# The last down block of eight experts: from 12 steps over 96 rows in the third part to 11 steps of 128 rows

## The chip, the cores and the metric

The kernel runs on one core of one Trainium2 chip. A core has TensorE (PE; its weight loads are listed apart as PEld), VectorE (DVE), ScalarE (ACT), GpSimd (POOL) and SyncE (SP), which here issues the transfers from HBM; 16 DMA engines move them. The metric is the device time of one execution in microseconds (us); the median of some runs is given. Inputs, weights and results are float32.

## The reference

Two transformer-like blocks follow each other on 256 tokens of width 1024. The first ends in 32 experts, the second holds two layers; the second of these ends in 8 experts of inner width 1408, two for each token, and only these matter here:

```python
def _swiglu(h, wg, wu, wd):
    return (jax.nn.silu(h @ wg) * (h @ wu)) @ wd

def _moe(h, router, wg, wu, wd):
    ...
    top_p, top_i = lax.top_k(probs, TOP_K_2)
    ...
    for e in range(N_EXPERTS_2):
        out = out + gates[:, e:e + 1] * _swiglu(hf, wg[e], wu[e], wd[e])
```

The kernel computes each expert only for the tokens that chose it.

## The kernel before

The program is one sequence of stages; the last one, `block2_moe` (from about 2340 us on), runs the 8 experts, with `moe_experts` (L979 on) as its loop. An expert has 96 places for tokens, in three groups of 32. Groups 0 and 1 always run. Group 2 stands under a condition (`tc.If`, L1081 and L1147) and runs only where an expert has more than 64 tokens; a branch jumps over its code otherwise. For an expert with more than 96 tokens there is `moe_rest`, which has the same arithmetic in other shapes and isn't entered in the profiled execution.

The inner width of 1408 is cut into four quarters of 352. A group's 32 tokens stand four times in the 128 columns of TensorE's array, one 32-column strip for each quarter (`tile_position=(0, 32 * q)`), so four products of 32 columns run side by side. For expert e the loop does:

- `gate_up` (L1058 on): gate and up products for each quarter, into `gu` (the first 256 of a quarter, L1071 with 512 moving columns) and `gub` (the remaining 96, L1071 with 192). Then the activation (L2268 to L2271) gives `a`, 128 x 3 x 352: row 32q + t is token t in quarter q.
- `combine(e - 2)` (L1041 to L1051): puts finished rows back to their tokens.
- `down(e - 1)` (L1119 on): the down products, L1140. The inner width is the contraction: a step takes one piece of one quarter, from `aT` as stationary and a row block `w` of down weights as moving operand, and issues four products, one for each 256 output columns. There are 8 steps with 128 rows (pieces 0 and 1 of the four quarters) and 4 with 96 rows (piece 2), so 12 for each group. The first four steps run for all groups, then the other eight.
- `turn(e)` (L1110 to L1117): transposes `a`, piece by piece, into PSUM (L1116) and copies it on ScalarE to `aT` (L1117); `aT` lies in `hTk`.

So experts are numbered from 0 here, and the down products of expert e stand after the gate and up products of expert e + 1.

Weights come in tiles through a ring of eight slots of 2 MB (`wtile`, L293 to L305, which issues the transfer). The slots are taken in a fixed order, so a transfer is issued when the last product on the tile eight places ahead is done. An expert takes nine tiles: gate and up in `wgu2` (four of 2 MB) and `wgu2b` (two of 1.5 MB, 128 rows of 12 KB), down in `wdn2` (two of 2 MB) and `wdn2b` (one of 1.5 MB: piece 2 of the four quarters, 96 rows of 16 KB). All are issued on SyncE's queue, in the order in which they are used. `load_dn` (L2278) lists the twelve steps: tile, block in the tile, quarter, piece.

Instructions of each engine are ordered by a scheduler when the program is built; the sections below show the places that matter. A float32 product stands as two passes in the trace, each with its weight load.

Of the kernel before, what the change touches and what calls it, by code (L numbers as in the profile page):

```python
# [13 lines left out]
AF = mybir.ActivationFunctionType  # L14
# [16 lines left out]
def host_layout(inp):  # L31
    f = lambda n: np.asarray(inp[n])
    c = np.ascontiguousarray
    o = {}
# [7 lines left out]
    w = f("w_in")[0]  # L42
# [21 lines left out]
    E = 32  # L64
# [11 lines left out]
    E = 8  # L76
# [2 lines left out]
    o["wgu2b"] = c(gu[..., 256:].reshape(E, 2, 4, 128, 768).transpose(0, 1, 3, 2, 4))  # L79
    wd = f("moe_w_down_2")[0].reshape(E, 4, 352, 1024)  # L80
    o["wdn2"] = c(wd[:, :, :256].reshape(E, 2, 4, 128, 1024).transpose(0, 1, 3, 2, 4))
    o["wdn2b"] = c(wd[:, :, 256:].transpose(0, 2, 1, 3))
    o["pos"] = c(f("positions_2").reshape(2, 128).T)
    w = f("w_in_2")
    rw = 1808
# [134 lines left out]
def bc(ap, shape):  # L220
    return ap.to_broadcast(shape)
# [71 lines left out]
def wtile(K, src, w=None):  # L293

    if w is None:
        if K.pre:
            return K.pre.pop(0)
        w = wslot(K)
    n = 1
    for s in src.shape[1:]:  # L300
        n *= s
    v = w[0:src.shape[0], 0:n]
    if len(src.shape) == 3:
        v = v.rearrange("p (a b) -> p a b", a=src.shape[1])
    K.nc.sync.dma_start(out=v, in_=src)  # L305
    return v
# [672 lines left out]
def moe_experts(K, pool, ps, mc, hs, cols, route, nE, F, load_gu, load_dn, bias, act, Y, cond, init):  # L979
# [4 lines left out]
    nc, tc = K.nc, K.tc  # L984
    nA = 256
    nB = F - nA
    pcs = [(0, 128), (128, 128)] + ([(256, nB)] if nB else [])
# [7 lines left out]
    two = 1 not in cond  # L995
# [57 lines left out]
    def start(p_, q, m, e=None):  # L1053

        l, r = (zl, bc(zl[:, 0:1], [96, m])) if e is None else (bc(bias[1][:, e:e + 1], [96, 32]), bias[0][:, 512 * q:512 * q + 512])
        nc.tensor.matmul(p_[32 * q:32 * q + 32, :], lhsT=l, rhs=r, start=True, stop=True, tile_position=(0, 32 * q))
# [53 lines left out]
    def turn(e):  # L1110
        a = st.pop(("a", e))
        aT = st["aT", e] = hTf[:, 0:384 * len(pcs)].rearrange("p (a b c) -> p a b c", a=len(pcs), b=3)
        for i, (o_, w_) in enumerate(pcs):
            pt = ps("x", [128, 3, 128])
            for g in range(3):
                nc.tensor.transpose(pt[0:w_, g, :], a[:, g, o_:o_ + w_], K.ident)  # L1116
            nc.scalar.activation(aT[0:w_, i], pt[0:w_], AF.Copy, scale=0.5)  # L1117

    def down(e):  # L1119
        aT = st.pop(("aT", e))  # L1120
        n = st.pop(("n", e))
        dn = load_dn(e)
        pd = [ps("d", [128, 2, 256]), ps("d", [128, 1, 256])]
        if bias is None:
            for p_, m in list(zip(pd, (512, 256)))[two:]:
                for c in range(4):
                    start(p_.rearrange("p a b -> p (a b)"), c, m)
        pd = [pd[0][:, 0], pd[0][:, 1], pd[1][:, 0]]
        if bias is not None:
            for g in range(3):  # L1130
                for c in range(4):
                    nc.tensor.matmul(pd[g][32 * c:32 * c + 32, :], lhsT=bc(bias[1][:, e:e + 1], [96, 32]),
                                     rhs=bias[2][c // 2][:, 256 * (c % 2):256 * (c % 2) + 256], start=g != 1, stop=True,
                                     tile_position=(0, 32 * c), skip_group_check=True)

        def part(g, dn, first):
            for k, (w, i, q, pi) in enumerate(dn):
                kk = pcs[pi][1]
                for c in range(4):
                    nc.tensor.matmul(pd[g][32 * c:32 * c + 32, :], lhsT=aT[0:kk, pi, g, 32 * q:32 * q + 32],  # L1140
                                     rhs=w[0:kk, i, 256 * c:256 * c + 256], start=first and two and g == 0 and k == 0, stop=True,
                                     tile_position=(0, 32 * c), skip_group_check=True)

        for n_, ds in enumerate((dn[:4], dn[4:]) if two else (dn,)):
            for g in range(3):
                if g in cond:
                    with tc.If(n > 32 * g):  # L1147
                        part(g, ds, n_ == 0)
                else:
                    part(g, ds, n_ == 0)  # L1150
        o = st["o", e] = [pool.tile([96, 1024], F32R, name=f"o{i}") for i in range(2)]
        rc = st["rc", e]
        of = pool.tile([96, 1024], F32, name="of") if nB else hTf[0:96, 1024:2048]
        for c in range(4):
            for g in range(3):
                dst, src, w_ = of[32 * g:32 * g + 32, 256 * c:256 * c + 256], pd[g][32 * c:32 * c + 32, :], rc[32 * g:32 * g + 32, 1:2]
                if g < 2:
                    nc.scalar.activation(dst, src, AF.Copy, scale=w_)  # L1158
                else:
                    nc.vector.tensor_scalar(dst, src, w_, None, op0=OP.mult)  # L1160
            if c % 2:
                c_ = slice(256 * c - 256, 256 * c + 256)
                if st["row"] is not None:
                    nc.vector.tensor_tensor(of[:, c_], of[:, c_], st["row"][0:96, c_], op=OP.mult)
                nc.scalar.activation(o[0][:, c_], of[:, c_], AF.Copy)  # L1165
                nc.vector.tensor_tensor(o[1][:, c_], of[:, c_], o[0][:, c_], op=OP.subtract)
# [4 lines left out]
    first = prep(0, range(4) if f32r else (0,))  # L1171
# [21 lines left out]
def moe_rest(K, pool, ps, h, cols, mc, posm, tgw, cnt, nE, F, wga, wgb, wda, wdb, bias, act, Y, row=None, after=None):  # L1193

    nc, tc = K.nc, K.tc
    nB = F - 256
    pcs = [(0, 128), (128, 128)] + ([(256, nB)] if nB else [])
# [3 lines left out]
    with tc.If(n > 96):  # L1201
        with tc.For_i(0, 2, 1):
            nc.vector.tensor_scalar(posm, posm, -96.0, None, op0=OP.add)
            with tc.For_i(0, nE, 1) as e:
# [14 lines left out]
                for q in range(2):  # L1219
                    px = ps("x", [128, 4, 96])  # L1220
                    for j in range(4):
                        for tt in range(2):
                            nc.tensor.matmul(px[:, j, :], lhsT=h[:, tt, 128 * (4 * q + j):128 * (4 * q + j) + 128], rhs=S[:, tt, 0, :],
                                             start=tt == 0, stop=tt == 1)
# [3 lines left out]
                a = pool.tile([96, 4, F], F32, name="a")  # L1228
                wa = [wtile(K, dyn(wga, e, i)) for i in range(4)]
                wb = [wtile(K, dyn(wgb, e, i)) for i in range(2)] if nB else []  # L1230
                for q in range(4):
# [9 lines left out]
                    if nB:  # L1241
                        pB = ps("gub", [96, 2 * nB])
                        for kt in range(8):
                            nc.tensor.matmul(pB, lhsT=xg[:, kt, :], rhs=wb[kt // 4][:, kt % 4, 2 * nB * q:2 * nB * q + 2 * nB],
                                             start=kt == 0, stop=kt == 7)
                        act(a[:, q, 256:F], pB[:, 0:nB], pB[:, nB:2 * nB], nB, 96)
                aT = hTf[:, 0:384 * len(pcs)].rearrange("p (a b c) -> p a b c", a=len(pcs), b=4)
                for i, (o_, w_) in enumerate(pcs):
                    pt = ps("x", [128, 4, 96])
                    for q in range(4):  # L1250
                        nc.tensor.transpose(pt[0:w_, q, :], a[:, q, o_:o_ + w_], K.ident[0:96, 0:96])
                    nc.scalar.activation(aT[0:w_, i], pt[0:w_], AF.Copy, scale=0.5)
                wd = [wtile(K, dyn(wda, e, i)) for i in range(2)]
                dn = [(wd[k // 4], k % 4, k // 2, k % 2, 128) for k in range(8)]
                if nB:
                    wl = wtile(K, dyn(wdb, e, None))
                    dn += [(wl, q, q, 2, nB) for q in range(4)]
                o = pool.tile([96, 1024], F32, name="of") if nB else hTf[0:96, 1024:2048]
                for c in range(2):
                    po = ps("d", [96, 512])  # L1260
                    for j, (w, i, q, pi, kk) in enumerate(dn):
                        nc.tensor.matmul(po, lhsT=aT[0:kk, pi, q, :], rhs=w[0:kk, i, 512 * c:512 * c + 512], start=j == 0,
                                         stop=j == len(dn) - 1)
                    o_ = o[:, 512 * c:512 * c + 512]
                    if row is None:
                        nc.scalar.activation(o_, po, AF.Copy)
                    else:
                        br = a.rearrange("p a b -> p (a b)")[:, 0:512]
                        nc.sync.dma_start(out=br, in_=bc(bias[1][bass.ds(e, 1), 512 * c:512 * c + 512], [96, 512]))
                        nc.vector.tensor_tensor(o_, po, br, op=OP.add)  # L1270
                        nc.vector.tensor_tensor(o_, o_, row[0:96, 512 * c:512 * c + 512], op=OP.mult)
# [10 lines left out]
def dyn(a, e, i):  # L1282

    if i is None:
        return a[bass.ds(e, 1)].rearrange("o p a b -> (o p) a b")
    return a[bass.ds(e, 1), i:i + 1].rearrange("o u p a b -> (o u p) a b")


def block1_moe(K, A):
# [65 lines left out]
    posm, tgw, num = moe_experts(K, pool, ps, mc, [h], mcol, route, 32, 256, load_gu, load_dn, (K.b3, K.oneh, bd), act, K.xres, (1, 2), row)  # L1355
    squares()
    moe_rest(K, pool, ps, h, mcol, mc, posm, tgw, num, 32, 256, A["wgu"], None, A["wdn"], None, (A["bgu"], A["bdn"]), act, K.xres, g2[0], squares)
    K.pend = [A["fnw"]]
    nc.vector.tensor_tensor(ssq, sq4[:, :, 0], sq4[:, :, 1], op=OP.add)
# [871 lines left out]
def block2_moe(K, A, out):  # L2231
    nc, tc = K.nc, K.tc
# [44 lines left out]

    def load_dn(e):  # L2278
        ws = [wtile(K, A["wdn2"][e, n]) for n in range(2)] + [wtile(K, A["wdn2b"][e])]
        return [(ws[k // 4], k % 4, k // 2, k % 2) for k in range(8)] + [(ws[2], q, q, 2) for q in range(4)]  # L2280

    moe_experts(K, pool, ps, mc, hs, K.lnc, route, 8, 352, load_gu, load_dn, None, act, Y, (2,), residual)
    moe_rest(K, pool, ps, K.xres, K.lnc, mc, *res, 8, 352, A["wgu2"], A["wgu2b"], A["wdn2"], A["wdn2b"], None, act, Y)
# [57 lines left out]
```

## Time and profile before

| | |
|---|---|
| median of 3 runs | 2742.53 us (2739.48 to 2747.18) |
| the profiled execution | 2748.39 us |
| its span, first to last instruction | 2746.6 us |
| TensorE busy | 2456.1 us (89% of the span) |
| VectorE, ScalarE, GpSimd busy | 1436.6, 935.7, 229.0 us |
| moved by DMA | 717.15 MB, 261 GB/s in the mean |
| TensorE's granted clock, mean | 0.953 of full speed |

The span is what the trace covers; 1.8 us of the profiled execution lie around it. An engine is busy while one of its instructions runs; matmuls are pipelined, so a busy TensorE needn't be at its peak. A pause is told with what ended it: another engine's instruction, a transfer (DMA), an engine's sequencer (PEq) or "issue", when nothing that the profile shows was waited for. DMA queue q1 carries the kernel's own transfers, q8 the packets of 16 KB with instructions.

### The profile page before, as it was taken

How to read it: one execution, taken by the hardware profiler on the slowest of the kernel's cores; microseconds unless marked ns; L12 is line 12 of the kernel's file. 1: busy time of each engine (PE TensorE's matmuls, PEld its weight loads, DVE VectorE, ACT ScalarE, POOL GpSimd, SP SyncE). 2: the span in 40 equal slices, each digit the busy share in tenths (PEclk: the TensorE clock that was granted, in tenths of full speed). 3: DMA queues.
4: the chain of work that ended last, by engine and by line, in shares of the span. 5: the costliest groups of instructions: out<-in, count | busy, mean ns of one | idle time of the engine just before them, and what ended most of it. 6: DMA issues, size and time to landing. Idle time of an engine off the chain costs nothing. (4 is left out here: it accounts for less than half of the span.)

```text
span 2746.6 us, 47587 instructions
## 1 busy us (share of the span) xinstructions
PE 2456.1 (89%) x20026; PEld 1610.0 (59%) x20026; DVE 1436.6 (52%) x2815; ACT 935.7 (34%) x1707; POOL 229.0 (8%) x222
## 2 busy tenths in 40 slices
PE   7999999988799989998997689879989987998895
PEld 4677668864344444443453278669987966554443
DVE  5888775554343454444343475775566577212223
ACT  4444344432132232222232362554444353021211
POOL 0422333110000000000000001110000030000000
PEclk9999999989999999999999799999999998999997
DMA  6333244759899999999999642345422225798994
GB/s 263 122 123 122 94 146 171 284 204 396 355 424 426 386 424 425 424 425 424 425 424 424 266 158 68 123 161 184 154 85 92 85 92 233 278 391 306 393 342 118
DMA packets 74282, 717.15 MB, mean 261 GB/s; under 512 B 9777, under 2 KB 25656, under 8 KB 29720
## 3 DMA queue, kind: packets, MB, share of 16 engines
q1 hardware_dynamic: 74008, 713.11, 66.1%
q8 instruction: 219, 3.59, 0.5%
q14 instruction: 55, 0.45, 0.0%
HBM read 712.03 MB, written 1.05 MB: 260 GB/s over the span
## 5 line engine op out<-in xcount | busy, mean ns | idle before, releaser
L1071 PE MATMUL gu<-w,xg 128*32 128x512 f32 x4400 | 539.7, 613 | 87.6 <-PEq L1081 48.0
L335 DVE TENSOR_TENSOR wlo<-w,whi 128x1024 fp32r<-128x1024 f32 (+1 forms) x250 | 309.1, 1238 | 206.5 <-ACT whi L334 205.4
L1071 PEld LDWEIGHTS gu<-w,xg 128*32 128x32 f32 x4400 | 157.2, 111 | 422.4 <-issue 369.8
L334 ACT ACTIVATE whi<-w 128x1024 fp32r<-128x1024 f32 (+1 forms) x250 | 260.7, 1045 | 380.9 <-PE pp L342 100.1
L1140 PE MATMUL d<-w,hTk 128*32 128x256 f32 (+1 forms) x5088 | 312.9, 392 | 30.7 <-issue 14.6
L1140 PEld LDWEIGHTS d<-w,hTk 128*32 128x32 f32 (+1 forms) x5088 | 178.8, 113 | 139.6 <-issue 53.8
L1330 DVE TENSOR_SCALAR a<-gu 128x256 f32<-128x256 f32 x96 | 39.5, 423 | 300.1 <-PE gu L1071 233.6
L1331 ACT ACTIVATE th<-a 128x256 f32<-128x256 f32 x96 | 36.6, 413 | 391.2 <-DVE a L1330 351.2
L1158 ACT ACTIVATE hTk<-d,rc 32x256 f32<-32x256 f32 x256 | 119.7, 468 | 79.3 <-PE d L1140 48.8
L1025 PE MATMUL x<-S,h 128*128 128x192 f32 (+2 forms) x608 | 110.7, 336 | 11.9 <-PEq L1147 4.9
L1049 PE MATMUL x<-o,R 96*128 96x512 f32 x320 | 95.5, 441 | 26.6 <-ACT o L1165 14.8
L1025 PEld LDWEIGHTS x<-S,h 128*128 128x128 f32 x608 | 99.0, 197 | 28.3 <-issue 18.2
L341 PE MATMUL pp<-big,whi 128*128 128x512 f32 (+2 forms) x296 | 110.0, 371 | 2.2 <-ACT big L473 2.2
L1117 ACT ACTIVATE hTk<-x 128x384 f32<-128x384 f32 (+1 forms) x88 | 41.0, 488 | 204.9 <-PE d L1140 138.6
L342 PE MATMUL pp<-big,whi 128*128 128x512 f32 (+2 forms) x296 | 109.4, 370 | 0.7 <-DVE big L474 0.5
L343 PE MATMUL pp<-big,wlo 128*128 128x512 f32 (+2 forms) x296 | 108.4, 367 | 0.0
L1049 PEld LDWEIGHTS x<-o,R 96*128 96x128 f32 x320 | 60.6, 203 | 73.7 <-issue 36.9
L341 PE MATMUL gu<-hT,whi 128*128 128x256 f32 x352 | 100.6, 286 | 1.9 <-ACT hT L2195 1.9
L343 PE MATMUL gu<-hT,wlo 128*128 128x256 f32 x352 | 100.5, 286 | 0.0
L342 PE MATMUL gu<-hT,whi 128*128 128x256 f32 x352 | 100.5, 286 | 0.0
L551 DVE SCALAR_TENSOR_TENSOR cacc<-pad,big,cacc 128x512 f32<-128x512 f32 (+1 forms) x128 | 98.0, 766 | 3.9 <-ACT cacc L548 1.2
L341 PE MATMUL pp<-whi,w 128*128 128x512 f32 (+1 forms) x192 | 81.3, 425 | 10.3 <-ACT w L2156 6.3
(734 smaller groups left out, 4701.6 us busy)
## 6 DMA issues: line engine op xcount, KB each, us to landing
w<-in_wgu_dram SPq DMA_DIRECT2D x155, 2048.0 KB, 22.7
w<-in_wdn_dram SPq DMA_DIRECT2D x80, 2048.0 KB, 25.9
w<-in_win_dram SPq DMA_DIRECT2D x18, 2048.0 KB, 7.9
w<-in_w2in_dram SPq DMA_DIRECT2D x30, 1024.0 KB, 5.2
w<-in_wgu2b_dram SPq DMA_DIRECT2D x16, 1536.0 KB, 15.3
w<-in_ffgu_dram SPq DMA_DIRECT2D x11, 2048.0 KB, 8.2
w<-in_wmod_dram SPq DMA_DIRECT2D x10, 2048.0 KB, 8.3
w<-in_wdn2b_dram SPq DMA_DIRECT2D x8, 1536.0 KB, 19.3
```

Source lines behind the costliest of these rows:

```text
L334: K.nc.scalar.activation(hi, src, AF.Copy)
L335: (eng or K.nc.vector).tensor_tensor(lo, src, hi, op=OP.subtract)
L341: K.nc.tensor.matmul(ps, lhsT=l[0], rhs=r[0], start=start, stop=False)
L342: K.nc.tensor.matmul(ps, lhsT=l[0], rhs=r[1], start=False, stop=False)
L343: K.nc.tensor.matmul(ps, lhsT=l[1], rhs=r[0], start=False, stop=stop)
L551: nc.vector.scalar_tensor_tensor(acc, pad[:, :S, k:k + 256], cw[:, ci, k:k + 1], acc, op0=OP.mult, op1=OP.add)
L1025: nc.tensor.matmul(px[:, j, :], lhsT=t_[:, tt, 128 * (q + j):128 * (q + j) + 128], rhs=S[:, tt, i:i + n].rearrange("p a b -> p (a b)"), st ...
L1049: nc.tensor.matmul(py, lhsT=R[:, 128 * tt:128 * tt + 128], rhs=o[i][:, 512 * c:512 * c + 512], start=i == 0, stop=i == 1)
L1071: mm = nc.tensor.matmul(p_[32 * q:32 * q + 32, :], lhsT=l_[:, kt, :], rhs=w[:, i, m * q:m * q + m], start=first, stop=True, tile_position= ...
L1117: nc.scalar.activation(aT[0:w_, i], pt[0:w_], AF.Copy, scale=0.5)
L1140: nc.tensor.matmul(pd[g][32 * c:32 * c + 32, :], lhsT=aT[0:kk, pi, g, 32 * q:32 * q + 32], rhs=w[0:kk, i, 256 * c:256 * c + 256], start=fi ...
L1158: nc.scalar.activation(dst, src, AF.Copy, scale=w_)
```

## The change

- On the host, the weights of the third pieces are laid out anew. Three quarters keep their 96 rows; the 96 rows of the fourth are cut into three blocks of 32, and each is put under one of the others. `wdn2b` becomes 128 rows of 12 KB instead of 96 rows of 16 KB, with the same bytes.
- `down` has 11 steps for each group, all of 128 rows.
- `turn` has to build the matching `aT`. The transposes of piece 2 stay, and their columns 96 to 127 (the fourth quarter) are no longer copied. For each group, three small products with 32 columns of `a` as stationary operand and 32 columns of the identity as moving operand put the fourth quarter's pieces into partitions 96 to 127, under the three others (`tile_position=(0, 96)`). The copy takes 128 x 3 x 96.
- `moe_rest` gets the same (left out below).

```diff
     o["wdn2"] = c(wd[:, :, :256].reshape(E, 2, 4, 128, 1024).transpose(0, 1, 3, 2, 4))
-    o["wdn2b"] = c(wd[:, :, 256:].transpose(0, 2, 1, 3))
+
+    o["wdn2b"] = c(np.concatenate([wd[:, :3, 256:], wd[:, 3, 256:].reshape(E, 3, 32, 1024)], 2).transpose(0, 2, 1, 3))
...
             pt = ps("x", [128, 3, 128])
             for g in range(3):
                 nc.tensor.transpose(pt[0:w_, g, :], a[:, g, o_:o_ + w_], K.ident)
-            nc.scalar.activation(aT[0:w_, i], pt[0:w_], AF.Copy, scale=0.5)
+                if i == 2:
+                    for j in range(3):
+                        nc.tensor.matmul(pt[96:128, g, 32 * j:32 * j + 32], lhsT=a[:, g, 256 + 32 * j:288 + 32 * j], rhs=K.ident[:, 96:128],
+                                         start=True, stop=True, tile_position=(0, 96))
+            c_ = 96 if i == 2 else 128
+            nc.scalar.activation(aT[:, i, :, 0:c_], pt[:, :, 0:c_], AF.Copy, scale=0.5)
...
             for k, (w, i, q, pi) in enumerate(dn):
-                kk = pcs[pi][1]
                 for c in range(4):
-                    nc.tensor.matmul(pd[g][32 * c:32 * c + 32, :], lhsT=aT[0:kk, pi, g, 32 * q:32 * q + 32],
-                                     rhs=w[0:kk, i, 256 * c:256 * c + 256], start=first and two and g == 0 and k == 0, stop=True,
+                    nc.tensor.matmul(pd[g][32 * c:32 * c + 32, :], lhsT=aT[:, pi, g, 32 * q:32 * q + 32],
+                                     rhs=w[:, i, 256 * c:256 * c + 256], start=first and two and g == 0 and k == 0, stop=True,
                                      tile_position=(0, 32 * c), skip_group_check=True)
...
-        return [(ws[k // 4], k % 4, k // 2, k % 2) for k in range(8)] + [(ws[2], q, q, 2) for q in range(4)]
+        return [(ws[k // 4], k % 4, k // 2, k % 2) for k in range(8)] + [(ws[2], q, q, 2) for q in range(3)]
```

The order on TensorE, second half of the down products of one expert, the transposes of the next one (piece 1 and 2) and the start of the gate products after it. `d` is the down sum, `x` the transposed piece, `gu` the gate and up sum; a row counts products, not passes; the row behind COMPARE_AND_BRANCH is group 2, which may be jumped over. Before:

```order
L1147 COMPARE_AND_BRANCH
L1140 MATMUL d<-w,hTk 32x256 x32
L1147 UNCONDITIONAL_BRANCH x2
L1140 MATMUL d<-w,hTk 32x256 x48
L1116 MATMUL x<-ident,a 128x128 x3
L1116 MATMUL x<-ident,a 96x128 x3
L1071 MATMUL gu<-w,xg 32x512 x32
L1081 COMPARE_AND_BRANCH
```

The same place in the changed kernel, where lines 1116 and 1140 are 1117 and 1145, and the small products line 1120:

```order
L1152 COMPARE_AND_BRANCH
L1145 MATMUL d<-w,hTk 32x256 x28
L1152 UNCONDITIONAL_BRANCH x2
L1145 MATMUL d<-w,hTk 32x256 x40
L1117 MATMUL x<-ident,a 128x128 x3
L1117 MATMUL x<-ident,a 96x128
L1120 MATMUL x<-ident,a 32x32 x3
L1117 MATMUL x<-ident,a 96x128
L1120 MATMUL x<-ident,a 32x32 x3
L1117 MATMUL x<-ident,a 96x128
L1120 MATMUL x<-ident,a 32x32 x3
L1072 MATMUL gu<-w,xg 32x512 x32
```

Each group has four down products fewer here (28 for 32 in group 2; 40 for 48 in the tail of group 0 and group 1), and three small products stand behind each transpose of piece 2. 

SyncE's queue, the tiles of two experts in turn (down of one, gate and up of the next but one). Before:

```order
L305 DMA w<-in_wdn_dram 128x4096
L1147 UNCONDITIONAL_BRANCH
L305 DMA w<-in_wdn2b_dram 96x4096
L305 DMA w<-in_wgu_dram 128x4096
L1147 UNCONDITIONAL_BRANCH
L305 DMA w<-in_wgu_dram 128x4096
```

In the changed kernel:

```order
L306 DMA w<-in_wdn_dram 128x4096
L1152 UNCONDITIONAL_BRANCH
L306 DMA w<-in_wdn2b_dram 128x3072
L306 DMA w<-in_wgu_dram 128x4096
L1152 UNCONDITIONAL_BRANCH
L306 DMA w<-in_wgu_dram 128x4096
```

The queue's order is the same; the block has 128 rows of 3072 elements instead of 96 rows of 4096.

## Rows read from the trace of the kernel before

**Rows 1.** Windows of 20 us: PE, PEld, DVE, ACT, POOL busy; clock, DMA share, GB/s.

```profile
2620.00:2640.00 20.00, 16.09 (x175) 8.00 (x177) 7.42 (x19) 1.27 (x4) 0.00 (x0) 0.76 0.99 277
2680.00:2700.00 20.00, 15.29 (x169) 7.97 (x168) 1.93 (x4) 3.19 (x7) 0.00 (x0) 0.74 0.94 254
```

**Rows 2.** Waits, TensorE alone, 2340 to 2705: total us, times, longest us.

```profile
PE d L1140 <- issue: 10.4, 5, 3.2
PE x L1049 <- issue: 7.3, 1, 7.3
...
PE d L1140 <- DMA w<-in_wdn2b_dram: 0.3, 1, 0.3
```

**Rows 3.** Timeline, TensorE: start us, us, work, count; in brackets the pause before it.

```profile
2440.12 2.25 PE L1049 MATMUL x<-o,R 96*128 96x512 f32 x8
...
2448.40 10.54 PE L1140 MATMUL d<-w,hTk 128*32 128x256 f32 x192
...
2487.32 3.57 PE L1049 MATMUL x<-o,R 96*128 96x512 f32 x8 [7.31 <-issue]
...
2491.01 6.70 PE L1140 MATMUL d<-w,hTk 128*32 128x256 f32 x96
...
2582.45 2.35 PE L1140 MATMUL d<-w,hTk 128*32 128x256 f32 x35 [0.64 <-DVE Y L1051]
2586.71 1.92 PE L1140 MATMUL d<-w,hTk 128*32 128x256 f32 x29 [1.91 <-issue]
...
2593.45 5.39 PE L1140 MATMUL d<-w,hTk 96*32 96x256 f32 x96 [2.42 <-PEq L1147]
...
2623.93 5.08 PE L1140 MATMUL d<-w,hTk 128*32 128x256 f32 x64 [1.76 <-DVE th L2270]
...
2633.01 0.64 PE L1140 MATMUL d<-w,hTk 128*32 128x256 f32 x7 [1.82 <-issue]
2633.94 8.60 PE L1140 MATMUL d<-w,hTk 96*32 96x256 f32 x96 [0.30 <-DMA w<-in_wdn2b_dram]
...
2680.17 2.42 PE L1140 MATMUL d<-w,hTk 128*32 128x256 f32 x32 [3.21 <-issue]
...
2688.48 8.64 PE L1140 MATMUL d<-w,hTk 96*32 96x256 f32 x96 [2.46 <-PEq L1147]
```

**Rows 4.** DMA view, 2471.9 to 2484.7 (its list of queues has only q1).

```profile
DMA packets 200, 2.80 MB, mean 219 GB/s; under 512 B 29, under 2 KB 29, under 8 KB 29
```

**Rows 5.** DMA view, 2484.7 to 2487.3: packets, MB, share of 16 engines' time.

```profile
q8 instruction: 1, 0.02, 3.2%
```

**Rows 6.** DMA view, 2382 to 2697, the instruction queue.

```profile
q8 instruction: 37, 0.61, 0.8%
```

**Rows 7.** Timeline, SyncE's queue, the block over 96 partitions of expert 3.

```profile
2528.63 0.33 SPq L305 DMA_DIRECT2D w<-in_wdn2b_dram  x1
```

**Rows 8.** DMA view, 2529.5 to 2537.3, the stretch after that issue.

```profile
DMA packets 130, 1.88 MB, mean 242 GB/s; under 512 B 15, under 2 KB 15, under 8 KB 15
```

**Rows 9.** DMA view, 2359.2 to 2362.9, a gate-up remainder (128 partitions, 12 KB).

```profile
DMA packets 130, 1.61 MB, mean 436 GB/s; under 512 B 16, under 2 KB 16, under 8 KB 16
```

**Rows 10.** DMA view, 2590.6 to 2593.4, while TensorE pauses for 2.42 us.

```profile
DMA packets 87, 1.18 MB, mean 420 GB/s; under 512 B 9, under 2 KB 9, under 8 KB 9
```

**Rows 11.** Lines, shapes apart: count, busy us, mean ns, idle before.

```profile
L1140 PE MATMUL d<-w,hTk 96*32 96x256 f32 x608 | 41.1, 406 | 5.4 <-PEq L1147 5.1 <-DMA w<-in_wdn2b_dram 0.3
...
L927 PE MATMUL x<-wr,hTk 128*128 128x32 f32 x32 | 3.8, 268 | 0.0
```

**Rows 12.** Timeline, TensorE, gate-up products and transposes in turn.

```profile
2521.71 0.55 PE L1116 MATMUL x<-ident,a 128*128 128x128 f32 x3
2522.19 1.06 PE L1071 MATMUL gu<-w,xg 128*32 128x512 f32 x8
2523.18 0.87 PE L1116 MATMUL x<-ident,a 128*128 128x128 f32 x6
2523.99 0.62 PE L1071 MATMUL gu<-w,xg 128*32 128x512 f32 x2
```

More of the change, by code (lines that the diff above doesn't have):

```diff
@@ L1249, in moe_rest @@
                     pt = ps("x", [128, 4, 96])
-                    for q in range(4):
+                    n_ = 3 if i == 2 else 4
+                    for q in range(n_):
                         nc.tensor.transpose(pt[0:w_, q, :], a[:, q, o_:o_ + w_], K.ident[0:96, 0:96])
-                    nc.scalar.activation(aT[0:w_, i], pt[0:w_], AF.Copy, scale=0.5)
+                        if i == 2:
+                            nc.tensor.matmul(pt[96:128, q, :], lhsT=a[:, 3, 256 + 32 * q:288 + 32 * q], rhs=K.ident[0:96, 0:96],
+                                             start=True, stop=True, tile_position=(0, 96))
+                    nc.scalar.activation(aT[:, i, 0:n_], pt[:, 0:n_], AF.Copy, scale=0.5)
                 wd = [wtile(K, dyn(wda, e, i)) for i in range(2)]
-                dn = [(wd[k // 4], k % 4, k // 2, k % 2, 128) for k in range(8)]
+                dn = [(wd[k // 4], k % 4, k // 2, k % 2) for k in range(8)]
                 if nB:
                     wl = wtile(K, dyn(wdb, e, None))
-                    dn += [(wl, q, q, 2, nB) for q in range(4)]
+                    dn += [(wl, q, q, 2) for q in range(3)]
                 o = pool.tile([96, 1024], F32, name="of") if nB else hTf[0:96, 1024:2048]
@@ L1260, in moe_rest @@
                     po = ps("d", [96, 512])
-                    for j, (w, i, q, pi, kk) in enumerate(dn):
-                        nc.tensor.matmul(po, lhsT=aT[0:kk, pi, q, :], rhs=w[0:kk, i, 512 * c:512 * c + 512], start=j == 0,
+                    for j, (w, i, q, pi) in enumerate(dn):
+                        nc.tensor.matmul(po, lhsT=aT[:, pi, q, :], rhs=w[:, i, 512 * c:512 * c + 512], start=j == 0,
                                          stop=j == len(dn) - 1)
```

## The prediction

> **What bounds the kernel now.** I read the windows of the last stage first (the second experts, from about 2340 us on), then TensorE's waits, then its timeline, then the DMA view in short stretches. Only differences in this stage count, since nothing ahead of it is touched.
>
> The windows show a stage in which the DMA engines are nearly full (shares 0.99 and 0.94) and TensorE is not: 16.09 and 15.29 us busy out of 20, at a mean granted clock of 0.76 and 0.74 [rows 1]. That looks like waiting for weights. The waits say otherwise: in 365 us TensorE waited 0.3 us for a weight transfer, but 10.4 us (5 times) and 7.3 us (once) under "issue", where nothing that the profile shows was missing [rows 2]. So weights are there in time, and something else stops it.
>
> The timeline shows where [rows 3]: pauses of 7.31, 1.91, 1.82 and 3.21 us under "issue", two of 2.42 and 2.46 us behind the branch of L1147, and 1.76 us ahead of the down products of expert 5 (2623.93), where expert 4 loses 0.64 us at the same place (2582.45). The pause of 1.91 us lies inside a run of equal products, after 35 of 64, where no operand changes. What ends such a pause is seen in the DMA view. In the 12.8 us up to 2484.7 the weight queue alone moved packets, and no instruction packet came [rows 4]; in the next 2.6 us exactly one did, of 0.02 MB, 3.2% of 16 engines' time, that is 1.3 us [rows 5], and TensorE went on at 2487.32. Over the stage 37 such packets came in 315 us, one in 8.5 us [rows 6]. I read this as: TensorE runs out of instructions, because the packet that brings the next ones stands behind weight packets on its DMA engine.
>
> Why there? The 1.5 MB block over 96 partitions is issued at 2528.63 [rows 7], and in the following 7.8 us the packets move 242 GB/s in the mean [rows 8]. A block of the same bytes over 128 partitions, the gate-up remainder, passes in 3.7 us at 436 GB/s [rows 9]. So a packet of the 96-partition block holds its engine about 1.8 times as long for its bytes, and what stands behind it waits longer. Stretches of the slow kind carry the long pause (219 GB/s in rows 4).
>
> **The change, part by part.**
>
> *The transfer.* Eight blocks take the shape of rows 9: 6.5 us (1.57 MB at 242 GB/s) or more become 3.7. The transfers themselves are no term, as weights are not waited for; the instruction packets behind them are. Pauses near such blocks: 7.31 + 1.91 + (1.76 - 0.64) + 1.82 + 3.21 + 2.46 = 17.8 us [rows 3]. [...] Its price comes from equal work at either level [rows 3]: 3.57 against 2.25 for the eight combining products; 6.70 against 5.39 for 96 down products (the latter at 2593.45); 5.08 against 3.59 (two thirds of 5.39); 8.60 and 8.64 against 5.39; 2.42 against 1.80: together 11.2 us. Both sum to 29.0 us.
>
> Not all of it goes. The pause of 2.42 us [rows 3] came while the DMA moved 420 GB/s [rows 10], and of the 10.4 us under "issue" 3.5 us lie outside slow stretches (10.4 - 1.91 - 1.82 - 3.21). I leave one pause of 2.4 us in experts 5 and 6 each, 4.8 us; after the one at 2593.45 the products ran at 5.39, full speed, so no clock loss is left with it. Back come 29.0 - 4.8 = **24.2 us**; as bounds, a third (9.7, if most of the waiting belongs to full queues of any packets) and all of it with the other pauses too (29.0 + 3.5 + 2.4 = 34.9).
>
> [...]
>
> *The removed step.* 19 of 24 expert groups run (608 / 32), and each loses one of four 96-row steps: 152 of 608 passes [rows 11]. At 10.54 us for 192 passes (0.055 us each) [rows 3] this takes 8.3 us from TensorE, all in its own chain.
>
> *The small products.* Three for each group, in all three groups of eight experts: 72 products. A product in float32 stands as two passes in the trace, so 144 passes of 32 columns. No row shows them. Below: 0.055 us, the rate of the column-tiled down passes; above: 0.119 us (3.8 / 32), 32 moving columns too, but with 128 columns of weights [rows 11]. These load 32, which is nearer to the first: 0.07 us, 10.1 us in all (bounds 7.9 and 17.1). They also alternate with full-width transposes. Three transposes take 0.48 us from start to the next product, six 0.81, so three more cost 0.33 and a change of layout there and back 0.15 [rows 12]. Two more such pairs for each expert: 2.4 us. [...]
>
> *The copy* of the third piece is 288 elements wide, not 384, on ScalarE, which stands outside TensorE's chain here; I count nothing. Nor does it cost if it comes to the front: a shorter copy takes the place of a longer one. *Issue order*: the queue of transfers keeps its order, row by row; only the shape differs. No wait is added. The last layer's tail, from 2705 on, loses its part of the removed passes, which is counted above.
>
> *Sum.* 24.2 back, 8.3 back, 10.1 and 2.4 spent: **20.0 us less**. The profiled execution, 2748.39 us, would become 2728; it lies 5.9 us above the median of the runs shown, and against that median, 2742.5, the forecast is **2722.5 us**.
>
> **The rivals.**
>
> *All pauses go.* With shorter transfers the queue is no longer full all the time, and instruction packets pass at once. For it: only slow stretches carry the pause of 7.31. Against: the 2.42 at 420 GB/s. With 34.9 back and the lower price of the products: 34.9 + 8.3 - 7.9 - 2.4 = 32.9, so 2709.6 us.
>
> *The pauses stay.* They belong to jumps over code that is not run (five groups are skipped) and to full queues, not to the block's shape. For it: two stand behind the branch of L1147. Against: 1.91 inside a straight run. Between none and a third comes back: 9.7 + 8.3 - 12.5 = 5.5 less, or 4.2 more: 2737 to 2747, say 2742. [...]
>
> *Slower: the products are dear.* All three of a group go to the same 32 columns and follow each other. If each pass must wait until the one before has left the array, it costs its whole duration, 0.268 us in the row with 32 moving columns [rows 11]: 38.6 us and 2.4 against 24.2 and 8.3, 8.5 us slower, 2751. It decides from 0.21 us a pass on ((24.2 + 8.3 - 2.4) / 144). Against it: the same row's passes follow at 0.119.
>
> *The change does not do what it says*: the block over 128 partitions stays slow, for its source rows are joined from two places. Rows 9 show this very shape at full rate, so I give it little; 2747.
>
> **How the numbers follow.** Chances: forecast 0.50, all pauses go 0.22, pauses stay 0.20, products dear 0.06, no effect on the transfer 0.02. Low end: all pauses go, 2709, and a little for unseen ones, 2708. High end: a third comes back with products at 0.119: 9.7 + 8.3 - 17.1 - 2.4, 1.5 us more, 2744. Beyond it lie the dear products and the worst part of "pauses stay". About 0.3%, 8.2 us, is what a measurement of this kernel can tell from no change. Faster by more: 0.50 + 0.22 and 0.04 from the edge of "pauses stay" = 0.76; slower by more: 0.06 and 0.01 of the last case = 0.07; the rest 0.17.
>
> **What would show it.** Right: the eight blocks move at over 400 GB/s; no pause over 3 us under "issue"; 20-us windows of the last experts with a granted clock near 1; 456 passes of the third kind of step, not 608. Steps wrong: blocks at full rate but the same pauses (the queue, not the shape); pauses gone but products at over 0.1 us a pass. The prediction is wrong if weights become what TensorE waits for, or if new pauses stand at the jumps.

## The result and the profile after

| | before | after |
|---|---|---|
| median | 2741.06 us (4 runs, 2739.48 to 2747.18) | 2712.14 us (4 runs, 2708.36 to 2715.85) |
| ratio to before | 1 | 0.9889 (95%: 0.9875 to 0.9903) |
| profiled execution, its span | 2748.39, 2746.6 us | 2715.85, 2713.9 us |

The changed kernel is 28.9 us faster by the medians, where 20.0 were forecast. The measured time lies inside the range, between the forecast (2722.5) and the rival "all pauses go" (2709.6). Lines moved a little: the down products of L1140 are L1145 now, the gate and up products L1072, the combining products L1050, the branch L1152, the small products L1120.

The windows that answer to [rows 1] (columns as there):

```profile
2480.00:2500.00 20.00, 18.67 (x205) 10.68 (x204) 6.95 (x17) 2.87 (x7) 0.00 (x0) 0.83 0.89 369
...
2600.00:2620.00 20.00, 18.96 (x293) 11.48 (x284) 8.26 (x21) 2.40 (x7) 0.00 (x0) 1.00 1.00 423
2620.00:2640.00 20.00, 19.59 (x252) 11.75 (x250) 1.38 (x2) 5.68 (x12) 0.00 (x0) 1.00 1.01 426
```

At 2620 TensorE is busy for 19.59 us of 20 instead of 16.09, its clock is granted in full instead of 0.76, and the DMA moves 426 GB/s instead of 277, at the same share of busy time. So the engines were no less busy before; they moved less.

TensorE's waits of the changed kernel, 2340 to 2672, against [rows 2] (total us, times, longest us):

```profile
PE d L1145 <- DVE Y L1052: 2.7, 4, 0.7
PE x L1050 <- ACT of L1163: 2.5, 1, 2.5
PE gub L1072 <- issue: 2.4, 1, 2.4
PE d L1145 <- issue: 1.7, 3, 1.2
PE d L1145 <- PEq L1152: 1.5, 5, 0.7
```

The 10.4 us of down products under "issue" are 1.7, the 7.3 us ahead of the combining products are gone, and the largest pause of that kind is one of 2.4 us, at 2479.67, at about the place of the former 7.31. Weights are still not waited for. In the timeline the down products of expert 4 behind the branch, formerly 2.42 us late [rows 3], are 0.19 late:

```profile
2577.56 0.55 PE L1117 MATMUL x<-ident,a 128*128 128x128 f32 x3
2578.04 0.27 PE L1057 MATMUL gub<-zl 96*32 96x192 bf16 x4
2578.13 1.90 PE L1145 MATMUL d<-w,hTk 128*32 128x256 f32 x32
2580.22 4.58 PE L1145 MATMUL d<-w,hTk 128*32 128x256 f32 x80 [0.19 <-PEq L1152]
2584.74 0.66 PE L1117 MATMUL x<-ident,a 128*128 128x128 f32 x4
2585.32 0.38 PE L1120 MATMUL x<-ident,a 128*32 128x32 f32 x6
2585.63 0.31 PE L1117 MATMUL x<-ident,a 128*96 128x128 f32 x1
2585.87 0.38 PE L1120 MATMUL x<-ident,a 128*32 128x32 f32 x6
2586.18 0.32 PE L1117 MATMUL x<-ident,a 128*96 128x128 f32 x1
2586.42 0.28 PE L1120 MATMUL x<-ident,a 128*32 128x32 f32 x3
2586.51 0.63 PE L1072 MATMUL gu<-w,xg 128*32 128x512 f32 x3
```

Behind it stand the new products, six passes, a transpose's pass, six passes again: from the first transpose to the next gate product 1.77 us, where six transposes alone took 0.81 [rows 12]. In the lines of 2280 to 2714, shapes apart (count, busy us, mean ns, idle before):

```profile
L1145 PE MATMUL d<-w,hTk 128*32 128x256 f32 x1672 | 99.1, 389 | 5.9 <-DVE Y L1052 2.7 <-issue 1.7 <-PEq L1152 1.5
L1120 PE MATMUL x<-ident,a 128*32 128x32 f32 x144 | 9.0, 200 | 0.0
```

1672 down passes are left of 1824 (608 of the third kind [rows 11] and 1216 others), 152 fewer, as counted; 144 small passes came. The 200 ns are the duration of one pass, not its pace: six took 0.38 us in the timeline above.

The block's own way in is told by the page's list of DMA issues (KB each, median us from issue to landing), before and after. It halves, though a landing holds the time in the queue too:

```profile
w<-in_wdn2b_dram SPq DMA_DIRECT2D x8, 1536.0 KB, 19.3
```

```profile
w<-in_wdn2b_dram SPq DMA_DIRECT2D x8, 1536.0 KB, 9.1
```

**One sum for all runs.** The stretch from the first to the last down product of these experts is called the stage here. From each trace I take its length, the sum of TensorE's pauses over 0.6 us, the part of them that ends 1.2 to 2.0 us after an instruction packet had come in, and the time at the lower granted clock (0.50 of full speed, as from 2488 to 2492 in the windows of the kernel before). Each is one execution. The one of the changed kernel was the longest of its four, and that of the kernel before lay 7.3 us above its median, so differences under 4 us or so are not read.

| kernel | stage | pauses | after an instruction packet | lower clock |
|---|---|---|---|---|
| before | 328.4 | 32.3 | 26.5 | 37.5 |
| after | 296.2 | 11.0 | 5.6 | 13.7 |
| e1 before, block padded | 305.0 | 18.3 | 12.5 | 13.7 |
| e2 after, block in 96 + 32 rows | 317.7 | 24.7 | 8.1 | 27.3 |
| e3 before, 4 KB packets | 325.6 | 33.4 | 25.5 | 30.7 |
| e4 after, no small products | 286.8 | 14.1 | 8.2 | 6.8 |
| e5 after, small products last | 291.7 | 11.8 | 5.3 | 10.2 |
| e7 after, half columns | 348.3 | 48.5 | 45.8 | 44.4 |
| e8 after, block padded | 298.0 | 12.8 | 6.8 | 10.2 |
| e9 after, block cut by rows | 317.0 | 27.1 | 10.5 | 20.5 |
| e10 after, block cut by columns | 292.5 | 10.5 | 5.5 | 6.8 |
| e11 after, cut by rows, partly interleaved | 316.5 | 21.6 | 11.9 | 27.3 |

At the lower clock equal work takes longer by 2.25 to 3.57 or 5.39 to 8.60 [rows 3], so 0.37 of that time is lost. The small products of expert 0 run ahead of the stage (from 2361 us on), so it holds those of seven experts. The change then reads: pauses 32.3 - 11.0 = 21.3 less, clock 23.8 x 0.37 = 8.8 less, removed passes 152 x 5.39 / 96 = 8.5 less, small products 7 x (1.77 - 0.81) = 6.7 more: 31.9 us less, of 32.2 measured in the stage.

### The profile page after: what moved, and what is told of

Read it like the earlier page. It is cut to its first block, busy times and chain, and to the rows that moved or that the text cites. A ratio compares the mean times of both kernels' runs of the same rounds, so it can differ in the third digit from the quotient of the medians.

```text
span 2713.9 us, 47571 instructions
## 1 busy us (share of the span) xinstructions
PE 2444.3 (90%) x20018; PEld 1626.4 (60%) x20018; DVE 1436.9 (53%) x2815; ACT 935.2 (34%) x1707; POOL 229.3 (8%) x222
## 3 DMA queue, kind: packets, MB, share of 16 engines
q8 instruction: 218, 3.57, 0.5%
## 5 line engine op out<-in xcount | busy, mean ns | idle before, releaser
L1072 PE MATMUL gu<-w,xg 128*32 128x512 f32 x4400 | 539.0, 612 | 87.9 <-PEq L1082 46.9
L1072 PEld LDWEIGHTS gu<-w,xg 128*32 128x32 f32 x4400 | 168.8, 111 | 409.1 <-issue 365.2
L1145 PE MATMUL d<-w,hTk 128*32 128x256 f32 x4936 | 295.2, 385 | 17.1 <-issue 6.3
L1145 PEld LDWEIGHTS d<-w,hTk 128*32 128x32 f32 x4936 | 172.6, 111 | 114.8 <-issue 32.6
L1026 PEld LDWEIGHTS x<-S,h 128*128 128x128 f32 x608 | 99.1, 197 | 28.7 <-issue 18.7
L1050 PE MATMUL x<-o,R 96*128 96x512 f32 x320 | 96.5, 443 | 18.3 <-ACT o L1170 14.8
L1050 PEld LDWEIGHTS x<-o,R 96*128 96x128 f32 x320 | 60.7, 205 | 66.7 <-issue 30.4
```

What stands on the lines that cost most here:

```text
L1026: nc.tensor.matmul(px[:, j, :], lhsT=t_[:, tt, 128 * (q + j):128 * (q + j) + 128], rhs=S[:, tt, i:i + n].rearrange("p a b -> p (a b)"), st ...
L1050: nc.tensor.matmul(py, lhsT=R[:, 128 * tt:128 * tt + 128], rhs=o[i][:, 512 * c:512 * c + 512], start=i == 0, stop=i == 1)
L1072: mm = nc.tensor.matmul(p_[32 * q:32 * q + 32, :], lhsT=l_[:, kt, :], rhs=w[:, i, m * q:m * q + m], start=first, stop=True, tile_position= ...
L1145: nc.tensor.matmul(pd[g][32 * c:32 * c + 32, :], lhsT=aT[:, pi, g, 32 * q:32 * q + 32], rhs=w[:, i, 256 * c:256 * c + 256], start=first an ...
```

## The experiments

All ratios are to the kernel before, run on the same chip.

**e1, the old kernel with a full-width block.** Only the transfer's shape changes: the 96 rows get 32 rows of zeros, so that 128 rows of 16 KB are fetched, a third more bytes. The steps stay twelve.

```diff
-    o["wdn2b"] = c(wd[:, :, 256:].transpose(0, 2, 1, 3))
+    o["wdn2b"] = c(np.pad(wd[:, :, 256:].transpose(0, 2, 1, 3), ((0, 0), (0, 32), (0, 0), (0, 0))))
```

> The kernel before, with all 12 steps and no small products, but its last down block is padded with 32 rows of zeros to 128 rows of 16 KB (2 MB), so that it moves in the fast shape. Theory A (instruction packets wait behind the slow packets of the 96-partition block, and TensorE runs dry and falls to the lower clock): pauses over 1 us nearly all go, granted clock near 1 in the last experts, some 28 us less than before, 2708 to 2718. Rival B (the gain came from TensorE's own work, 11 steps for 12): no change, 2737 to 2745. Rival C (the length of the weight transfers themselves counts): 4.9 us for the block in place of some 7.3, against 3.7 in the changed kernel, so about two thirds of the gain, 2719 to 2725.

Measured: 2723.76 us (2719.14 to 2727.11), 0.9928 (0.991 to 0.9946); 19.8 us of the 28.9. That is above the 2708 to 2718 of theory A and inside the 2719 to 2725 of rival C, which goes by the block's bytes; e8 below tests that. The shape is not all of the gain. More bytes went in less time: 11.9 us from issue to landing in the median, where it was 19.3. In the stage pauses fall by 14.0, all of it among those after instruction packets (26.5 to 12.5), and the lower clock takes 23.8 us x 0.37 = 8.8 less: 22.8 of the 23.4 us by which the stage is shorter. The 7.31 us became this (timeline of the padded kernel):

```profile
2474.70 1.84 PE L1071 MATMUL gub<-w,xg 128*32 128x192 f32 x40
2479.48 3.41 PE L1049 MATMUL x<-o,R 96*128 96x512 f32 x8 [2.95 <-issue]
```

Its windows show TensorE at its full clock, the DMA at 421 GB/s:

```profile
2620.00:2640.00 20.00, 17.96 (x246) 8.34 (x241) 1.38 (x2) 6.24 (x13) 0.00 (x0) 1.00 1.00 421
```

So the shape alone, with no change in the computation, carries about two thirds of the gain. What is left can be seen: 12.5 us of pauses after instruction packets are left, the changed kernel has 5.6.

**e2, the changed kernel with the block cut into 96 and 32 rows.**

```diff
-        ws = [wtile(K, A["wdn2"][e, n]) for n in range(2)] + [wtile(K, A["wdn2b"][e])]
+        ws = [wtile(K, A["wdn2"][e, n]) for n in range(2)] + [wslot(K)[:, 0:3072].rearrange("p (a b) -> p a b", a=3)]
+        for p in (slice(0, 96), slice(96, 128)):
+            K.nc.sync.dma_start(out=ws[2][p], in_=A["wdn2b"][e][p])
```

> The changed kernel, with 11 steps and small products, but its last down block (128 rows of 12 KB) is fetched by two transfers, 96 rows and then 32 rows. Theory A: both reach only some of the partitions and move slowly again, pauses behind them return, 2728 to 2742 (a packet is 12 KB here, not 16, so somewhat less than all). Rival B (11 steps for 12): stays at the changed kernel's time, 2709 to 2716. Rival C: as A.

Measured: 2733.91 us (10 runs, 2726.37 to 2748.92), 0.997 (0.9952 to 0.9988): two thirds of the gain by the medians, nearly three quarters by the ratios, are lost by this alone. Most of the loss has another form than before (TensorE's waits, 2340 to 2692):

```profile
PE d L1145 <- DMA w<-in_wdn2b_dram: 7.6, 2, 4.8
PE d L1145 <- issue: 4.9, 4, 2.2
```

Now the weights themselves are late, twice; before it was 0.3 us [rows 2]. Of the 13.7 us by which the pauses in the stage grow over the changed kernel's, only 2.5 end after an instruction packet. So the pauses that theory A expected came back only in small part; 7.6 us of waiting for the block came in their place. I read it so: TensorE comes to the block earlier, and the block is as slow as before (247 GB/s in the DMA view of 2525 to 2532, against 242 in [rows 8]). The slow block cost in two ways: in the kernel before 26.5 us of pauses after instruction packets and 0.3 us of waiting for it, here 8.1 us (5.6 in the changed kernel) and 7.6 us. That TensorE's pace decides between them is not shown by itself.

**e3, the old kernel with packets of 4 KB in place of 16 KB.** The block keeps its 96 rows and its bytes; if a number of packets ahead in the queue made the instructions late, four times as many would change it.

```diff
-    o["wdn2b"] = c(wd[:, :, 256:].transpose(0, 2, 1, 3))
+    o["wdn2b"] = c(wd[:, :, 256:])
...
-        return a[bass.ds(e, 1)].rearrange("o p a b -> (o p) a b")
+        return a[bass.ds(e, 1)].rearrange("o q p b -> p (o q) b")
...
-        ws = [wtile(K, A["wdn2"][e, n]) for n in range(2)] + [wtile(K, A["wdn2b"][e])]
+        ws = [wtile(K, A["wdn2"][e, n]) for n in range(2)] + [wtile(K, A["wdn2b"][e].rearrange("q p b -> p q b"))]
```

> The kernel before, with 12 steps and the 96-partition block, whose rows are laid out in HBM by quarter, so that one transfer has four packets of 4 KB for each partition in place of one of 16 KB. Theory A, if an instruction packet waits for a number of packets ahead of it: the block stays slow (200 to 250 GB/s), but the wait behind it is a quarter as long, pauses go, 2710 to 2722. If it waits for the block's bytes whatever their packets: pauses stay, 2735 to 2745. Rival C (length of the transfer): 2735 to 2745 with the pauses of before. Rival B: 2737 to 2745.

Measured: 2743.96 us, 0.9999 (0.9985 to 1.0013), no change. The block passes at the old rate (DMA view, 2470 to 2480; 219 GB/s in [rows 4]), and the long pauses stand where they stood, 6.4 us the longest:

```profile
DMA packets 416, 2.19 MB, mean 219 GB/s; under 512 B 25, under 2 KB 25, under 8 KB 368
```

The pauses sum up to 33.4 us, against 32.3 before. So here it didn't matter into how many packets the block's bytes were cut; they moved at the same rate, and the pauses stayed.

**e4 and e5, the small products.** e4 leaves them out, and with them the last 96 channels of the fourth quarter from the sums. e5 issues all nine behind the three transposes instead of three behind each. Their edits:

```diff
-                if i == 2:
-                    for j in range(3):
-                        nc.tensor.matmul(pt[96:128, g, 32 * j:32 * j + 32], lhsT=a[:, g, 256 + 32 * j:288 + 32 * j], rhs=K.ident[:, 96:128],
-                                         start=True, stop=True, tile_position=(0, 96))
...
-            nc.scalar.activation(aT[:, i, :, 0:c_], pt[:, :, 0:c_], AF.Copy, scale=0.5)
+            nc.scalar.activation(aT[0:w_, i, :, 0:c_], pt[0:w_, :, 0:c_], AF.Copy, scale=0.5)
```

```diff
             for g in range(3):
                 nc.tensor.transpose(pt[0:w_, g, :], a[:, g, o_:o_ + w_], K.ident)
-                if i == 2:
+            if i == 2:
+                for g in range(3):
                     for j in range(3):
```

> The changed kernel without the 72 small products (it leaves out placing the fourth quarter's last 96 channels). The prediction's price for them, 10.1 + 2.4 us: 2700. By the changed kernel's trace (passes 0.03 us apart, but a change of layout of over 0.1 us at each side of a transpose) some 9 us: 2701 to 2705. If they are hidden beside other work: 2709 to 2714.

> The changed kernel with the nine small products of an expert behind its three transposes of the third piece, not three behind each: two changes of layout there and back less for each expert. The changed kernel's trace has some 0.13 us more at each change between them: 0.5 us an expert, 4 us in all, 2706 to 2710. The prediction's 0.15 us a pair: 2.4 us less, about 2710. If a change of layout costs nothing by itself: 2712.

Measured: e4 2707.5 us (2702.92 to 2709.36), 0.9861 (0.9845 to 0.9878); e5 2705.49 us (2703.5 to 2712.1), 0.9852 (0.9835 to 0.9868). e4 lies between its two cases (2701 to 2705, and 2709 to 2714 if the products were hidden), e5 just below its 2706 to 2710. Moving the products brings as much as leaving them out, within the intervals, and e5 is the fastest kernel of this study that computes all. Its timeline shows the same place as above:

```profile
2581.30 0.88 PE L1117 MATMUL x<-ident,a 128*128 128x128 f32 x6
2582.11 0.66 PE L1121 MATMUL x<-ident,a 128*32 128x32 f32 x15
2582.58 0.63 PE L1072 MATMUL gu<-w,xg 128*32 128x512 f32 x3
2582.60 0.26 PE L1121 MATMUL x<-ident,a 128*32 128x32 f32 x3
```

From the first transpose to the next gate product it is 1.28 us, not 1.77. The eighteen passes cost 1.28 - 0.81 = 0.47 us, 0.026 us each. They start 0.03 us apart (fifteen in 0.66 us, at 0.20 us for one), but the last three stand beside the first gate products. The two further pairs of layout changes in the changed kernel cost the other 0.49, 0.24 us a pair. Eight times over that is 3.8 us for the passes and 3.9 for the order.

**e7, twice as many instructions for the down products.** Each is cut into two of 128 columns. The weights, their transfers and the arithmetic stay, and each product still has its own weight load (3344 passes and 3344 loads in the lines). The sums lie 0.069 off (relative), for a reason that no run shows.

```diff
-                for c in range(4):
-                    nc.tensor.matmul(pd[g][32 * c:32 * c + 32, :], lhsT=aT[:, pi, g, 32 * q:32 * q + 32],
-                                     rhs=w[:, i, 256 * c:256 * c + 256], start=first and two and g == 0 and k == 0, stop=True,
+                m = 256 if bias is not None else 128
+                for o_, c in [(o_, c) for o_ in range(0, 256, m) for c in range(4)]:
+                    nc.tensor.matmul(pd[g][32 * c:32 * c + 32, o_:o_ + m], lhsT=aT[:, pi, g, 32 * q:32 * q + 32],
+                                     rhs=w[:, i, 256 * c + o_:256 * c + o_ + m], start=first and two and g == 0 and k == 0, stop=True,
```

> The changed kernel with each down product of the second experts cut into two of 128 columns: the same arithmetic and the same transfers, twice the instructions in the down steps. Theory A (TensorE runs out of instructions, whose packets wait in full queues): long pauses come back in every expert, ended by instruction packets, 2735 to 2780. If pauses come from weights or from branches, not from the supply of instructions: passes of 128 columns follow each other at no less than 0.03 us, so the work does not grow, 2705 to 2720.

Measured: 2765.73 us (2764.56 to 2769.82), 1.0079 (1.0062 to 1.0095), 53.6 us above the changed kernel. The products themselves take 115.7 us instead of 99.1, part of it at the lower clock; but in front of them stand 43.2 us of pauses under "issue" and the branch (lines, 2280 to 2763):

```profile
L1146 PE MATMUL d<-w,hTk 128*32 128x128 f32 x3344 | 115.7, 299 | 45.9 <-issue 27.9 <-PEq L1153 15.3 <-DVE Y L1052 2.5
```

In its timeline TensorE stops in the middle of equal products:

```profile
2396.28 5.08 PE L1146 MATMUL d<-w,hTk 128*32 128x128 f32 x128 [3.50 <-issue]
2403.32 3.78 PE L1146 MATMUL d<-w,hTk 128*32 128x128 f32 x127 [1.95 <-issue]
2409.36 2.35 PE L1146 MATMUL d<-w,hTk 128*32 128x128 f32 x38 [2.26 <-issue]
```

In the stage, pauses rise by 37.5 and the lower clock by 30.7 x 0.37 = 11.4 us, 48.9 of 52.1. Data, transfers and multiplications are the same, only the number of instructions changed, and 45.8 of the 48.5 us of pauses ended 1.2 to 2.0 us after an instruction packet: I read these pauses as a lack of instructions. 128 and 127 passes stand between the pauses above, each pause ended by one more packet; they took 5.08 and 3.78 us.

The records of the packets, each with its start, say how far apart they come. In e7 the packets that ended pauses over 1 us ahead of or inside runs of down products started 5.6 to 8.9 us after the one before (the first and the last of these pauses aside), while the DMA moved 381 to 438 GB/s. In the kernel before, those that ended the pauses of 7.31, 1.91, 1.82, 3.21 and 2.46 us came 13.9, 10.2, 9.5, 16.4 and 9.0 us after the one before, at 205 to 278 GB/s. 128 passes of 256 columns take 7.2 us (at 5.39 us for 96). So at the full rate a packet came about as often as 128 of these are done, and too seldom for passes of 128 columns (5.08 and 3.78 us for 128 and 127); at the slow rate of the kernel before it came too seldom for passes of 256 columns as well. That a packet stands behind weight packets on its engine is not shown, as the traces don't name the engine of a packet; that the packets came further apart where the queue moved slower is.

Pauses of this kind came even with next to no weights to move. Towards the end of e7's stage, with the DMA at a share of 0.02, a packet came 3.0 us after the one before and still ended a pause (window and timeline):

```profile
2704.00:2710.00 6.00, 4.95 (x143) 4.08 (x138) 2.43 (x6) 0.06 (x1) 0.00 (x0) 1.00 0.02 5
```

```profile
2710.73 3.48 PE L1146 MATMUL d<-w,hTk 128*32 128x128 f32 x118 [1.60 <-issue]
```

**e8, the changed kernel with the block padded to 2 MB.** e1 fetches a third more bytes than the changed kernel and keeps more pauses. Are the bytes the reason?

```diff
+    o["wdn2b"] = c(np.pad(o["wdn2b"], ((0, 0), (0, 0), (0, 1), (0, 0))))
```

> The changed kernel, its block padded with a fourth, unused column block to 128 rows of 16 KB (2 MB): the transfer of the padded kernel with 11 steps. If the transfer's bytes made the padded kernel's remaining pauses (rival C in its weaker form: fuller queues): pauses over 0.6 us as there (18.3 us), 2717 to 2723. If they come from the longer code of 12 steps: as the changed kernel, 2709 to 2715.

Measured: 2716.13 us (2711.67 to 2720.56), 0.9893 (0.9875 to 0.9912), as the changed kernel and a little above the 2709 to 2715 expected for that. Not the bytes, then, and rival C falls. What e1 alone has among the kernels whose block moves at full rate is the twelfth step: it keeps 12.5 us of pauses after instruction packets, the five with eleven steps (after, e4, e5, e8, e10) 5.3 to 8.2, with the small products or without.

**e9, e10, e11: what makes the block slow.** e9 cuts the changed kernel's block by rows in another way for each expert (64 + 64, 96 + 32, 112 + 16, four times 32, 32 + 96, 80 + 48, and whole for experts 0 and 7), with a loop like e2's; e10 cuts it by columns, 128 rows of 8 KB and of 4 KB; e11 by rows again, now also interleaved. e10's edit, and e11's list of cuts in the place of e2's:

```diff
-            K.nc.sync.dma_start(out=ws[2][p], in_=A["wdn2b"][e][p])
+        for p in (slice(0, 2), slice(2, 3)):
+            K.nc.sync.dma_start(out=ws[2][:, p], in_=A["wdn2b"][e][:, p])
```

```diff
+        for p in ((slice(0, 128),), (slice(0, 128, 2), slice(1, 128, 2)), (slice(0, 64), slice(64, 128)), (slice(0, 128, 4), slice(1, 128, 4), slice(2, 128, 4), slice(3, 128, 4)),
+                  (slice(0, 120), slice(120, 128)), (slice(0, 128, 2), slice(1, 128, 2)), (slice(0, 64), slice(64, 128)), (slice(0, 128),))[e]:
```

> The changed kernel with the block of each expert fetched over other partition counts: 128; 64 + 64; 96 + 32; 112 + 16; four times 32; 32 + 96; 80 + 48; 128. One look, for the rates. [...] If it follows what the 96-partition block showed: 96 at some 210 to 240 GB/s. Time between 2715 and 2740.

> The changed kernel, its last down block fetched in two transfers as in the split by rows, but cut by columns: 128 rows of 8 KB, then 128 rows of 4 KB. If a transfer is slow because it covers fewer than 128 partitions, both parts move at over 400 GB/s, stretches of 20 us show no share of 12 us at 200 to 260 GB/s, and the time is the changed kernel's, 2707 to 2720. If it is two transfers into one tile that are slow, or the second issue, the block moves at 200 to 260 GB/s again and the time is that of the split by rows, 2726 to 2740.

> The changed kernel, its last down block cut by rows in another way for each expert: 0 whole; 1 even and odd rows; 2 rows 0 to 63 and 64 to 127; 3 every fourth row, four times; 4 rows 0 to 119 and 120 to 127; 5 as 1; 6 as 2; 7 whole. If it is the span of partitions that makes a part slow (which of them lie together), the even and odd rows of experts 1, 3 and 5 reach all of the span and pass at over 400 GB/s with 0.46 us for a packet of 12 KB, and those of 2 and 6 take 0.8 us and more. If it is the number of rows of a transfer, 64 and 32 rows are slow in every order, 0.8 to 1.0 us a packet at 200 to 260 GB/s; 120 and 8 rows then also. Whole blocks: 0.46 us in either case. One look; time between 2720 and 2740 by the second, 2712 to 2728 by the first.

Measured: e9 2735.8 us and e11 2730.58 us in one execution each (before: 2745.68 and 2743.0 in the median); e10 2711.26 us (2709.42 to 2716.61), 0.9892 (0.9875 to 0.9908), the changed kernel's time. In e9 all six cuts are slow: a 12 KB packet takes 0.79 to 0.93 us in the median of each cut block, against 0.46 for the whole ones. In e10 none is, so a second transfer into the tile cost nothing that shows (0.9892 of the time before, against 0.9889 of the changed kernel). e11 separates the rest (DMA view, in this order: expert 2, rows 0 to 63 and 64 to 127, 2463 to 2469; expert 4, 120 and 8 rows, 2566 to 2572; expert 1, even and odd rows, 2417.5 to 2421.5):

```profile
DMA packets 127, 1.26 MB, mean 210 GB/s; under 512 B 29, under 2 KB 29, under 8 KB 29
...
DMA packets 106, 1.26 MB, mean 210 GB/s; under 512 B 8, under 2 KB 8, under 8 KB 8
...
DMA packets 165, 1.66 MB, mean 416 GB/s; under 512 B 35, under 2 KB 35, under 8 KB 35
```

64 rows that lie together moved at 210 GB/s, 64 rows that reach over all 128 partitions at 416; every fourth row, 32 in a transfer, took 0.46 us a packet too. So in these transfers it was not how many rows one has, but how they lie. 120 rows together were as slow as 64, 210 GB/s. The time of e11, 2730.58 us, lies above the 2712 to 2728 expected for this answer and inside the range of the other, with three of the eight blocks slow; the packets decide, not the one time.

## Why the prediction held, and where it was off

**What bounds the stage: right.** Of 32.3 us of pauses 26.5 ended after an instruction packet, and TensorE waited 0.3 us for weights. e7 shows such pauses by the number of instructions alone (45.8 us), e1 that the block's shape accounts for 14.0 of the 26.5. e2 shows that the shape brings a cost back, there mostly as waiting for the weights (7.6 us). The stretch of [rows 9] holds 62 packets of the remainder and 52 of a full-width tile, not the remainder alone; both kinds ran at the full rate (0.46 us for 12 KB, 0.61 for 16 KB), so the factor of 1.8 against [rows 8], where a 16 KB packet took 1.13 us, stands.

Nor do the jumps alone pay: in e7, at a DMA share of 0.85 in the mean (windows, 2394 to 2690), 27.9 us of waiting under "issue" stand ahead of or inside straight runs of down products, and 15.3 us behind the branch.

**The transfer's term: right in size, for the shape.** 24.2 us were forecast; the shape alone gave 19.8 by the medians and 23.4 in the stage (e1). Of that the clock is 8.8; the prediction had 11.2 for it, the price of the lower granted clock behind the pauses, from equal work at either level in [rows 3]. The pauses left, 12.5 us after instruction packets, are near what the prediction left standing (4.8 and the 3.5 and 2.4 of its upper bound, 10.7).

**What was missed: more pauses went than the shape accounts for.** The removed step was priced at 8.3 us of passes, and the passes fit (8.5). But with eleven steps 7.3 us more of pauses went than with e1's twelve. The step of the prediction that failed is "I leave one pause of 2.4 us in experts 5 and 6 each": under "issue" and behind the branch their down products now lose 0.60 and 0.18 us in all (timeline of the changed kernel), and those of expert 4, whose 2.42 us were left too, 0.19:

```profile
2616.08 4.48 PE L1145 MATMUL d<-w,hTk 128*32 128x256 f32 x75 [0.19 <-PEq L1152]
2620.97 0.63 PE L1145 MATMUL d<-w,hTk 128*32 128x256 f32 x5 [0.41 <-issue]
...
2661.31 4.52 PE L1145 MATMUL d<-w,hTk 128*32 128x256 f32 x80 [0.18 <-PEq L1152]
```

e1 keeps one of 2.04 us in expert 5. e8 excludes the bytes as the reason, e4 the small products. A down pass comes every 0.056 us (5.39 for 96 [rows 3]). That a shorter run of them leaves more time for the next packet is a reading that fits e7, but no run here changed the number of steps alone, and the cause of these 7.3 us stays open.

**The small products: right in kind, too dear.** A pass costs 0.026 us and starts 0.03 us after the one before, below the lower bound of 0.055 that was taken from the down passes; a pair of layout changes 0.24, above the 0.15 of [rows 12]. Together 7.7 us for 12.5. The nearest row for the pace was of passes with 256 columns; for products with 32 columns it was no lower bound. So in the stage pauses and clock gave 30.1 us for the 24.2 forecast, passes 8.5 for 8.3, and the small products of seven experts cost 6.7 for 12.5: 11.9 of the 12.2 us between the 20.0 forecast and the 32.2 in the stage. All three errors went the same way; none hid another.

**The rivals.** "All pauses go" gave 2709.6, the nearest number, but not for its reason: the full queue stayed (426 GB/s at a share of 1.01) and so did 5.6 us of pauses. "The pauses stay" fell with e1. "The products are dear" wanted 0.21 us a pass; it cost 0.026. "The change does not do what it says" fell with 426 GB/s and the landing time of 9.1 us. The copy cost nothing that shows.

## What to carry to other kernels

When TensorE stands still under "issue" or behind a branch, look into the DMA view for what came in just before: here instruction packets came 9.0 to 16.4 us apart ahead of the long pauses, while the weights moved at 205 to 278 GB/s. Give a weight block rows on all 128 partitions in each transfer, even at the cost of padding: a third more bytes took 20 us off here (e1). Where an order is free, put products of one tile layout together; here that alone was worth 2712.14 - 2705.49 = 6.7 us by the medians (10 by the ratios, each to the kernel before on its own chip), of which 3.9 are accounted for by the rows.

## What the hardware showed that was not expected

- Every cut into blocks of neighbouring rows ran at about half the rate, whatever its sizes, from four times 32 to 120 + 8: 0.79 to 0.96 us for a packet of 12 KB (e9, e11), in place of 0.46. The prediction had expected a factor of 1.8 from one shape, but not that 120 rows together would be as slow as 64, at 210 GB/s, where even and odd rows moved at 416. Why is left open.
- While a slow part passed, the 16 KB packets of full-width tiles beside it were slow as well: 1.15 us and more in the median beside each cut block of e9, in place of 0.61, and the whole queue moved at 191 to 237 GB/s (DMA view, one stretch of 7 to 12 us for each of the six cut blocks).
- A pause ended after an instruction packet even with the weight queue all but empty: 1.60 us in e7 at a share of 0.02. With the DMA at 381 to 438 GB/s, the packets that ended its pauses came 5.6 us and more after the one before.
